# Second product of both MLPs by Strassen's scheme: seven block products for eight, z in one chunk of operands

## The chip, the cores and the metric

The kernel runs on one core of one Trainium2 chip. The metric is the device time of one execution in microseconds (us). A core has four computing engines: TensorE (PE; its weight loads are listed as PEld), VectorE (DVE), ScalarE (ACT) and GpSimd (POOL). SyncE (SP) issues most of the DMAs. Each engine executes its own instructions in the order of the program and waits on semaphores for the others. In the profile, L128 is line 128 of the kernel.

## The reference

The kernel computes a two-layer encoder trunk on x of shape (1, 512, 1024), in float32. Layer 0 has a dilated window attention as its mixer, layer 1 a short gated convolution. After each mixer stands an MLP:

```python
def mlp_sq_relu(h, w1, w2):
    return jnp.square(jax.nn.relu(h @ w1)) @ w2

for i in range(DEPTH):                      # DEPTH = 2
    y = rms_norm(h, norm1[i])
    y = mixer_a(...) if kind == 0 else mixer_b(...)
    h = h + y
    h = h + mlp_sq_relu(rms_norm(h, norm2[i]), mlp_w1[i], mlp_w2[i])
```

`w1` is 1024 x 4096 and `w2` 4096 x 1024. The change concerns the second product of the two MLPs, `z @ w2` with z = square(relu(...)).

## The kernel before

**Split operands.** A float32 factor is held as two parts of type float32r, hi (the value rounded to that type) and lo (the rest). A product is three matmuls: hi x hi, hi x lo, lo x hi, summed in PSUM. For a weight tile of 128 x 512 the pair is made on chip by `split` (lines 289 to 296): ACT casts the loaded tile `wraw` into `wh` (L292), then POOL subtracts to make `wl` (L293).

**Units and blocks.** `add_unit` (L111) describes a product of four output tiles (PSUM banks, 128 x 512) by eight k-tiles of weights (128 x 512 each). It is cut into blocks of two k-tiles. A block of a full unit is 4 tiles x 2 k-tiles x 3 = 24 matmuls; each k-tile has one load and one split. When the last matmul of a tile is issued, `done` is called, which evacuates the bank. The matmuls are those of L128.

**The order of the work.** The program is written once, by the loop at the end (lines 966 to 978). `clock` counts positions, not time: a unit of 512 columns is 8 long, a block of two k-tiles 2. Every other operation is a task at a position (`at`, and `after` for "so much after now"); tasks are issued, in order of position, between the matmuls. Within an engine that is also the order of execution. Ahead of each block the loop issues the splits of weights that lie up to six k-tiles after the block's first (`NW = 6` buffers for wh and wl) and the loads of four more (`NRAW = 4` buffers). A split therefore waits for the matmuls that last read its buffers.

```python
for i, b in enumerate(blocks):
    run_tasks(b["start"] - 0.5)
    prep_to(b["first"] + min(NW, 2 * b["n"] + i // 4))
    load_to(nprep[0] + NRAW)
    run_tasks(b["start"])
    ops = b["emit"](...)
```

**The MLP.** z has 4096 features, worked on in four chunks c of 1024. `u1(u)` is one unit of the first product: four tiles of z, 128 features x 512 tokens each. `u1_done` evacuates each: DVE multiplies relu by the norm's factor R (zr, L794), ACT squares it (zz, L795) and casts it to hi (L796), DVE subtracts for lo (L797). There are two sets of z operands, so a chunk's second product comes one chunk later than its first: u1 0 to 3, then u2 of chunk 0, u1 4 and 5, u2 of chunk 1, and so on. `u2(c, half)` is one unit of the second product, for 512 of the 1024 output features: 96 matmuls of 512 columns. `u2_done` adds its banks into the tile `acc` (L809 for the first chunk, L811 for the others). In the last chunk the sum goes to the trunk tile `hT` (L813), and `new_h` makes from it the operands and squares of the next norm (L705 to L707, L704). Before that, `acc` takes up the trunk (L850).

In layer 0 (`last` false) the weight is the stationary operand and z moves, so the output has features on the partitions. In layer 1 (`last` true) z is stationary and the weight moves, so the output has tokens on the partitions, as the result in memory wants; the trunk is transposed by 32 PE transposes (L858) and added in L860, and the output leaves by DMA from L818 and L819.

Between layers `sums` (lines 710 to 722) adds the squares over the partitions by two matmuls (L717, L718), placed 2.8 positions after the last block.

The diff touches these functions:

## Time and profile before

| | |
|---|---|
| time, median of 3 runs (lowest, highest) | 1515.11 us (1514.34, 1516.41) |
| the profiled execution, its own time | 1515.53 us |
| its span in the profile | 1513.6 us |
| busy: PE, DVE, ACT, POOL | 98%, 47%, 44%, 47% |
| second product of the MLPs, in matmuls | 2 x 768, all 128x512 |
| data read from memory | 134.89 MB |

The span is what the profile covers; the time of the profiled execution is 1.9 us more. The duration printed for a matmul overlaps its neighbours', so the time that a stream of them takes is read from the distance between starts. A line of the timeline gives the start, the duration, engine, source line, operation, output and inputs, shape and count, and in brackets how long the engine had been idle and who ended that. A line of groups gives the count, the busy time, the mean in ns of one, and the idle time before them with what ended it. A line of a stretch of time gives its length, the busy time (and count) of PE, PEld, DVE, ACT and POOL, then the granted TensorE clock, the share of the DMA engines and GB/s.

### The profile page before, as it was taken

The page shows a single profiled execution, that of the slowest core. Times are in us where ns is not written, and L with a number is a line of the kernel's source. Part 1 is how long each engine was busy: PE and PEld are TensorE (multiplying, and loading weights), DVE is VectorE, ACT ScalarE, POOL GpSimd, SP SyncE. Part 2 cuts the span into 40 slices and gives each one's busy share as a digit, 9 for nine tenths or more (in the row PEclk, how much of TensorE's full clock was granted, in tenths as well). Part 3 has the DMA queues.
Part 4 walks back from the last instruction along what each step waited for, and adds up shares of the span by engine and source line. Part 5 has one row for each costly group of instructions (what it writes and reads, how often), then busy time and mean ns, then how long its engine had stood idle before and what let it go on. Part 6 is the DMA issues. An engine that isn't in the chain of part 4 may idle for free.

```text
span 1513.6 us, 22622 instructions
## 1 busy us (share of the span) xinstructions
PE 1483.0 (98%) x7900; PEld 1293.4 (85%) x7900; DVE 706.4 (47%) x1553; ACT 664.8 (44%) x1364; POOL 716.4 (47%) x729
## 2 busy tenths in 40 slices
PE   9899999999999998999999999999999999999998
PEld 8799999999999987888888888888887888888887
DVE  4867767776767665643012223564447330122221
ACT  6456564556556564444333332433343443333320
POOL 4454444536354553554444445454454444444442
PEclk9899999999999999999999999999999999999999
DMA  6332322323132323222222232233332223222222
GB/s 151 126 112 63 102 79 86 91 75 102 53 115 60 102 84 127 103 98 96 99 97 98 91 103 96 81 90 99 98 111 84 98 92 102 97 96 94 99 90 84
DMA packets 163294, 144.77 MB, mean 96 GB/s; under 512 B 13748, under 2 KB 123116, under 8 KB 163180
## 3 DMA queue, kind: packets, MB, share of 16 engines
q1 hardware_dynamic: 162892, 143.06, 30.1%
q8 instruction: 62, 1.02, 0.3%
q14 instruction: 52, 0.43, 0.1%
q10 hardware_dynamic: 288, 0.27, 0.1%
HBM read 134.89 MB, written 8.39 MB: 95 GB/s over the span
## 4 chain that ended last, share of the span: by engine, by line
PE 77%; DVE 11%; issue 5%; POOL 3%; ACT 2%; DMA 1%; SPq 1%; POOLq 0%; ACTq 0%; DVEq 0%
PE g L128 72%; PE st L461 1%; PE o L548 1%; PE st L520 1%; PE st L391 1%; POOL wl L293 1%; DMA wraw<-in_a_wqkv 1%; DVE sm L451 1%; DVE rawA L373 1%; DVE ptl L293 1%; DVE stA L156 1%; DVE stA L155 1%; DVE sqa L704 1%; SPq L571 1%; ACT wh L292 0%
## 5 line engine op out<-in xcount | busy, mean ns | idle before, releaser
L293 POOL TENSOR_TENSOR wl<-wraw,wh 128x512 fp32r<-128x512 f32 (+1 forms) x542 | 638.2, 1198 | 712.2 <-ACT wh L292 701.2
L292 ACT CAST wh<-wraw 128x512 fp32r<-128x512 f32 (+1 forms) x542 | 300.8, 572 | 528.1 <-PE g L128 405.7
L128 PE MATMUL g<-hgBl,wh 128*128 128x512 f32 x704 | 274.8, 390 | 0.0
L128 PE MATMUL g<-hgBh,wl 128*128 128x512 f32 x704 | 274.6, 390 | 0.0
L128 PE MATMUL g<-hgBh,wh 128*128 128x512 f32 x704 | 274.6, 390 | 0.0
L128 PE MATMUL g<-wh,hgl 128*128 128x384 f32 x768 | 267.7, 349 | 0.5 <-DVE hgl L307 0.4
L128 PE MATMUL g<-wh,hgh 128*128 128x384 f32 x768 | 262.4, 342 | 1.6 <-DVE v L296 1.6
L128 PE MATMUL g<-wl,hgh 128*128 128x384 f32 x768 | 262.7, 342 | 0.0
L794 DVE SCALAR_TENSOR_TENSOR zr<-g,R 128x512 f32<-128x512 f32 x64 | 44.2, 691 | 293.4 <-PE g L128 293.3
L128 PEld LDWEIGHTS g<-hgBh,wl 128*128 128x128 f32 x704 | 132.7, 189 | 27.7
L128 PEld LDWEIGHTS g<-hgBh,wh 128*128 128x128 f32 x704 | 132.6, 188 | 27.9
L128 PEld LDWEIGHTS g<-hgBl,wh 128*128 128x128 f32 x704 | 132.7, 189 | 27.4
L128 PEld LDWEIGHTS g<-wh,hgl 128*128 128x128 f32 x768 | 145.3, 189 | 3.6 <-DVE hgl L307 1.6
L128 PEld LDWEIGHTS g<-wh,hgh 128*128 128x128 f32 x768 | 145.2, 189 | 2.7 <-DVE v L296 2.2
L128 PEld LDWEIGHTS g<-wl,hgh 128*128 128x128 f32 x768 | 144.9, 189 | 0.5
L811 DVE TENSOR_TENSOR acc<-g,acc 128x512 f32<-128x512 f32 x32 | 22.1, 692 | 138.2 <-PE g L128 138.2
L128 PE MATMUL g<-z0h,wh 128*128 128x512 f32 x192 | 74.7, 389 | 0.0
L128 PE MATMUL g<-z0l,wh 128*128 128x512 f32 x192 | 74.7, 389 | 0.0
L128 PE MATMUL g<-z0h,wl 128*128 128x512 f32 x192 | 74.7, 389 | 0.0
L470 ACT ACTIVATE sm<-sm,mxs 128x256 f32<-128x256 f32 x128 | 64.0, 501 | 15.1 <-DVE mxs L464 11.6
L292 ACT CAST pth<-st 128x512 fp32r<-128x512 f32 x64 | 37.6, 588 | 66.7 <-PE st L520 66.4
L293 DVE TENSOR_TENSOR ptl<-st,pth 128x512 fp32r<-128x512 f32 x64 | 43.5, 688 | 27.8 <-ACT pth L292 27.8
(222 smaller groups left out, 2379.0 us busy)
## 6 DMA issues: line engine op xcount, KB each, us to landing
wraw<-in_mlp_w SPq DMA_DIRECT2D x256, 256.0 KB
wraw<-in_a_wqkv SPq DMA_DIRECT2D x128, 128.0 KB
wraw<-in_a_wqkv SPq DMA_DIRECT2D x64, 192.0 KB
wraw<-in_a_wqkv SPq DMA_DIRECT2D x128, 64.0 KB
wraw<-in_b_win SPq DMA_DIRECT2D x64, 128.0 KB
v0d<-v SPq DMA_DIRECT2D x8, 512.0 KB
v<-v0d SPq DMA_DIRECT2D x64, 64.0 KB
wraw<-in_a_wo SPq DMA_DIRECT2D x16, 256.0 KB
```

The lines of the kernel that those rows point to most:

```text
L128: pe.matmul(unit["ps"][n][:, :width], a, b, start=st, stop=sp)
L155: dve.tensor_mul(t, y, y)
L156: dve.scalar_tensor_tensor(t, t, -0.5, v, op0=ALU.mult, op1=ALU.mult)
L292: act.copy(hi, src)
L293: (eng or dve).tensor_sub(lo, src, f32(hi))
L373: dve.tensor_mul(v, v, stt[:, 2, ng * r:ng * r + ng, None].to_broadcast([128, ng, 64]))
L391: pe.transpose(o, raw[r][:, w, :], ident)
L451: dve.tensor_tensor_reduce(out=sm0[:, h, b], in0=ps[h][:, 256 * b2:256 * b2 + 256], in1=msk0[:, (0, 1, 1, 2)[b]], scale=1.0, scalar=3.0e38 ...
L461: pe.matmul(pv[:, :, g], a[:, 128 * r:128 * r + 128], k[:, 256 * r:256 * r + 256], start=(q == 0), stop=(q == 2))
L470: act.activation(t[:, h, b], t[:, h, b], AF.Exp, bias=mx(m)[:, c], scale=-1.0, accum_out=mx(d)[:, c])
L794: dve.scalar_tensor_tensor(zr, ps, 0.0, state["R"], op0=ALU.max, op1=ALU.mult)
L811: dve.tensor_add(a, ps, a)
```

## The change

The second product of a chunk is a product of a 2 x 2 block matrix by another: two halves of the chunk's features (row tiles of 128 taken alternately) by two halves of the output features, and two halves of the tokens (256 each). Before, that is eight block products. The change does it by Strassen's scheme in the form with shared sums: seven block products of sums of blocks, the results added into the right output blocks.

- *Order.* A chunk is now two units of the first product and then, at once, its seven products (`add_wino`). There is one set of z operands, `zh[i]` and `zl[i]` for i = 0 to 3, each holding seven forms of 256 columns: three plain quarters and four sums. Product q uses form `OPS[q]`. Each product is two blocks, of two of the four k-tiles i, in `ORDER`: 1, 5, 1, 5, 6, 6, 2, 2, 7, 7, 3, 3, 4, 4. A block is 12 matmuls of 512 columns in layer 1 and 24 of 256 in layer 0.
- *z.* `u1_done` works on two tiles together: ACT squares into V; DVE makes four sums of 256 columns in W (`zs`, one buffer); ACT casts three quarters and then the four sums; DVE subtracts for the low part of the quarters, POOL for that of the sums.
- *Weights.* A chunk still loads 16 tiles, into twelve tiles of their own (`quad`) and four of `wraw`, and forms the sums of blocks in place by 16 DVE subtractions (`quad_make`). It splits 28 tiles, 24 with the subtraction on POOL and four on DVE.
- *Results.* Products 1, 5 and 6 are summed over the chunks in `part` and go into the trunk at the end; 2, 3, 4 and 7 are added to the trunk tile (now one tile `HT`) as they end, 7 into two blocks. `acc` is gone. Layer 1's transposes are made in its first chunk, and the trunk is kept in that form.

```diff
+    OPS = {1: 0, 6: 4, 5: 3, 2: 2, 7: 5, 3: 6, 4: 1}
+    ORDER = [(1, 0), (5, 0), (1, 1), (5, 1), (6, 0), (6, 1), (2, 0), (2, 1), (7, 0), (7, 1), (3, 0), (3, 1), (4, 0), (4, 1)]
...
+    def quad_make(q, i, raw, held):
+        a, b, c = (t[i] for t in state["quad"])
+        if q == 5:
+            dve.tensor_sub(a, b, a)
+        elif q == 6:
+            dve.tensor_sub(a, c, a)
+        elif q == 2:
+            held[i] = raw
+            return raw, (dve if i % 2 else pool)
+        elif q == 7:
+            dve.tensor_sub(b, c, b)
+            return b, pool
+        elif q == 3:
+            return c, (dve if i % 2 else pool)
+        elif q == 4:
+            d = held.pop(i)
+            dve.tensor_sub(d, d, a)
+            return d, pool
+        return a, pool
...
+    def add_wino(w, c, tok, done):
+        banks, held = {}, {}
+        for q, half in ORDER:
+            def emit(ws, q=q, half=half):
+                if half == 0:
+                    banks[q] = [ps_m(0) for _ in range(2)]
...
+                for j in range(2):
+                    ps = banks[q][j]
+                    for e, (wh, wl) in enumerate(ws):
+                        i = 2 * half + e
+                        hi, lo = state["zh"][i][:, OPS[q]], state["zl"][i][:, OPS[q]]
...
+                        if tok:
+                            ah, al = hi[:, 128 * j:128 * j + 128], lo[:, 128 * j:128 * j + 128]
+                            todo = [(ps, ah, wh), (ps, ah, wl), (ps, al, wh)]
+                        else:
+                            for n in range(2):
+                                o = ps[:, 256 * n:256 * n + 256]
+                                bh, bl = (t[:, 256 * j + 128 * n:256 * j + 128 * n + 128] for t in (wh, wl))
+                                todo += [(o, bh, hi), (o, bh, lo), (o, bl, hi)]
...
         def u1_done(u):
             def f(n, ps):
+                i = 2 * (u % 2) + n // 2
+                H, L = state["zh"][i], state["zl"][i]
                 zr = ptile(state["tp"], [128, S], F32, "zr")
                 dve.scalar_tensor_tensor(zr, ps, 0.0, state["R"], op0=ALU.max, op1=ALU.mult)
-                after(0.4, lambda: act.activation(zz, zr, AF.Square))
-                after(0.6, lambda: act.copy(hi, zz))
-                after(0.9, lambda: dve.tensor_sub(lo, zz, f32(hi)))
+                e = 2 * (n % 2)
+                if e == 0:
+                    state["zz"] = ptile(state["tp"], [128, 4, 256], F32, "zz")
+                V = state["zz"]
+                after(0.4, lambda: act.activation(V[:, e:e + 2].rearrange("p a c -> p (a c)"), zr, AF.Square))
+                if e == 0:
+                    return
+                W = ptile(state["tp"], [128, 4, 256], F32, "zs", bufs=1)
+
+                def sums_z():
+                    dve.tensor_add(W[:, 0], V[:, 0], V[:, 2])
+                    dve.tensor_sub(W[:, 1], W[:, 0], V[:, 1])
+                    dve.tensor_sub(W[:, 2], V[:, 1], V[:, 0])
+                    dve.tensor_sub(W[:, 3], V[:, 3], W[:, 1])
+                after(0.5, lambda: act.copy(H[:, 0:3], V[:, 1:4]))
+                after(0.6, sums_z)
+                after(0.75, lambda: act.copy(H[:, 3:7], W))
+                after(0.9, lambda: dve.tensor_sub(L[:, 0:3], V[:, 1:4], f32(H[:, 0:3])))
+                after(1.0, lambda: pool.tensor_sub(L[:, 3:7], W, f32(H[:, 3:7])))
             return f
...
+        def u2_done(c):
+            def f(q, j, ps):
+                part = state["part"]
+                if q in part:
+                    v = part[q][:, j]
+                    if c == 0:
+                        act.copy(v, ps)
+                    else:
+                        dve.tensor_add(v, ps, v)
+                    if c == 3 and q == 6:
+                        a1, a5 = part[1][:, j], part[5][:, j]
+                        def both():
+                            pool.tensor_add(v, v, a1)
+                            pool.tensor_add(a5, a5, v)
+                        def more():
+                            for row, col, w in ((2, 2, a5), (1, 2, a5), (2, 1, v)):
+                                o = out_block(row, col, j)
+                                dve.tensor_add(o, o, shaped(w))
+                        o = out_block(1, 1, j)
+                        dve.tensor_add(o, o, shaped(a1))
+                        after(0.1, both)
+                        after(1.0, more)
+                    return
...
-        for u in range(4):
-            u1(u)
-        u2(0, 0)
-        u2(0, 1)
...
+        for c in range(4):
             u1(2 * c)
             u1(2 * c + 1)
+            add_wino(w2[layer], c, last, u2_done(c))
```

More of the change, by code (lines that the diff above doesn't have):

```diff
@@ L136, in add_unit @@
             for kt in blk:
[L137 removed]
+                loads.append((cols, lambda kt=kt: load_raw(load, kt), lambda raw: (raw, pool)))
     ident = ptile(const, [128, 128], F32, "ident")
@@ new lines, in mlp, with turn, back @@
+        if last:
+            for f in range(2):
+                box = {}
+                def turn(r, f=f, box=box):
+                    box[r] = ps_m(0)
+                    for q in range(4):
+                        pe.transpose(box[r][:, 128 * q:128 * q + 128], state["hT"][4 * f + q][:, 128 * r:128 * r + 128], ident)
+                def back(r, f=f, box=box):
+                    dve.tensor_copy(state["hT"][4 * f + r], box[r])
+                for r in range(4):
+                    at(t0 + 9.0 + 0.5 * r + 8.0 * f, lambda r=r, turn=turn: turn(r))
+                    at(t0 + 11.0 + 0.3 * r + 8.0 * f, lambda r=r, back=back: back(r))
@@ L946, in load_to @@
             k = nload[0]
-            raws[k] = ptile(wp, [128, 512], F32, "wraw", bufs=NRAW)
-            loads[k][1](raws[k])
+            raws[k] = loads[k][1]()
             nload[0] += 1
```

131 lines of the change are left out of this document (67 added, 64 removed).

## The prediction

> **What bounds the kernel now.** I read the page's first part, then the 40 slices, the waits of TensorE and two stretches of the timeline.
>
> ```profile
> span 1513.6 us, 22622 instructions
> PE 1483.0 (98%) x7900; PEld 1293.4 (85%) x7900; DVE 706.4 (47%) x1553; ACT 664.8 (44%) x1364; POOL 716.4 (47%) x729
> PE g L717 <- ACT sgh L292: 3.3, 1, 3.3
> 672.00:715.00 43.00, 43.00 (x192) 35.59 (x191) 12.24 (x16) 18.69 (x32) 20.69 (x16) 1.00 0.29 99
> 715.00:757.00 42.00, 42.00 (x187) 34.79 (x186) 2.19 (x2) 13.92 (x24) 19.89 (x16) 1.00 0.29 100
> ```
>
> PE is the bound: 98% busy, its longest wait in the MLPs is 3.3 us before layer 1, and a stretch of first products (672 to 715) or of second products (715 to 757) has PE busy throughout at clock 1.00, POOL at half. So a matmul fewer is time saved, as long as the other engines keep PE fed. What a matmul occupies is the distance between starts, not the printed duration:
>
> ```profile
> 999.72 0.39 PE L128 MATMUL g<-hgBl,wh 128*128 128x512 f32 x1
> 1003.80 0.39 PE L128 MATMUL g<-hgBl,wh 128*128 128x512 f32 x1
> ...
> 300.94 0.34 PE L128 MATMUL g<-wl,hgh 128*128 128x384 f32 x1
> 302.32 0.34 PE L128 MATMUL g<-wh,hgh 128*128 128x384 f32 x1
> ...
> 566.31 0.30 PE L461 MATMUL st<-k1h,q1h 128*128 128x256 f32 x1
> 566.44 0.28 PE L461 MATMUL st<-k1l,q1h 128*128 128x256 f32 x1
> 566.92 0.28 PE L461 MATMUL st<-k2h,q2l 128*128 128x256 f32 x1
> ```
>
> 512 columns: 18 steps in 4.08 us, 0.2267 each. 256 columns, every one with new weights, as the change has them: 4 steps in 0.48, 0.120 each. 384 columns lie on the same line: 8 steps in 1.38, 0.1725 each.
>
> **PE's own saving.** A layer's second product is 4 chunks x 2 halves x 4 tiles x 8 k-tiles x 3 = 768 matmuls of 512: 174.1 us. In layer 0 it becomes 4 x 7 x 48 = 1344 matmuls of 256: 161.3, so 12.8 saved. In layer 1 it becomes 672 of 512: 152.3, so 21.8 saved. Together 34.6. The 256 price is bounded by 0.113 (half of 0.2267) below and by 0.13 above (the first step, 566.31 to 566.44), −9 to +13 us; I take the row, because its matmuls have the same shape. The Trainium skill (TensorE: Matmul & The Clock Gate, Back-to-back issue gap) gives N/2.4 + 2.5 ns, 109 ns for 256 columns, by which layer 0 would save 27.4. The trace disagrees: the formula gives 216 for 512, where the rows have 227.
>
> **What the other engines pay.** A chunk's weights took 16 splits (ACT cast, then POOL or DVE subtraction); now 28, with 16 DVE subtractions to form sums of blocks. A PE block has two splits and lasts 12 x 0.2267 = 2.72 us in layer 1 (24 x 0.120 = 2.88 in layer 0), half of before.
>
> ```profile
> L293 POOL TENSOR_TENSOR wl<-wraw,wh x542: 992/1288/1760, 12.6 to 1494.2; 128x512 fp32r<-128x512 f32 x96, 128x384 fp32r<-128x384 f32 x85
> 652.31 1.76 POOL L293 TENSOR_TENSOR wl<-wraw,wh 128x512 fp32r<-128x512 f32 x1
> 746.04 2.54 POOL L293 TENSOR_TENSOR wl<-wraw,wh 128x512 fp32r<-128x512 f32 x2 [2.90 <-ACT wh L292]
> L292 ACT CAST wh<-wraw 128x512 fp32r<-128x512 f32 x288 | 175.2, 621 | 400.9 <-PE g L128 360.2 <-POOL wl L293 19.8 <-DVE zr L817 7.6
> L292 ACT CAST wh<-wraw 128x384 fp32r<-128x384 f32 x254 | 125.7, 516 | 127.1 <-PE g L128 45.6 <-issue 35.6 <-DMA wraw<-in_a_wqkv 31.1
> L795 ACT ACTIVATE zz<-zr 128x512 f32<-128x512 f32 x64 | 40.5, 633 | 30.8 <-DVE zr L794 28.7
> L794 DVE SCALAR_TENSOR_TENSOR zr<-g,R 128x512 f32<-128x512 f32 x64 | 44.2, 691 | 293.4 <-PE g L128 293.3
> L902 DVE TENSOR_TENSOR z0l<-sqh,z0h 128x512 fp32r<-128x512 f32 x8 | 5.5, 693 | 5.5 <-ACT z0h L901 5.5
> L960 DVE TENSOR_TENSOR wl<-wraw,wh 128x384 fp32r<-128x384 f32 x2 | 1.1, 558 | 0.1
> L811 DVE TENSOR_TENSOR acc<-g,acc 128x512 f32<-128x512 f32 x32 | 22.1, 692 | 138.2 <-PE g L128 138.2
> 931.77 2.77 DVE L850 TENSOR_TENSOR acc<-acc,hT 128x512 f32<-128x512 f32 x2
> 418.35 3.43 DMA wraw<-in_a_wqkv
> ```
>
> Alone, a POOL subtraction takes 1.27 (2.54 for two), a DVE one 0.69. Side by side, both reading two SBUF tiles, they slow each other: POOL 1.76, DVE 1.39 (2.77 for two). DVE with a PSUM input (L811) doesn't. By the slopes between 384 and 512 columns, estimates from these rows: DVE 256 columns 0.42, 768 0.96; ACT 768 0.83, 1024 1.04; POOL 1024 2.48 (1288 plus four times 296).
>
> Loads stay 16 of 256 KB a chunk. The second block's four are held in wraw to the seventh product, so on SP's queue the next unit's loads wait for those splits; product 4's first two end 0.7 + 0.6 + 2.5 = 3.8 us after block 10 begins, a load takes up to 3.4 us more, cast and split 1.9: 9.1, and the unit begins at 10.9. So this costs nothing. The other ACT casts, DVE evacuations (16 for 8, 0.69 each in 38 us) and L850's eight adds, now gone, lie beside PE: nothing. Layer 1's transposes move a chunk earlier at the same PE cost: nothing.
>
> **The step on the path: z becomes ready too late.** Before, a chunk's z was used one pair of units later. Now the chunk's products follow its last first-product unit at once. Products 1 and 5 on k-tiles 0 and 1 (blocks 0, 1) cover it; block 2 needs the last z tile in its first form, block 3 in its sums. The queues are in order, so I walk them; T = 0 where the unit's last PSUM tile is ready, layer 1:
> - Tile 1 is ready at −2.72: zr to −2.03, square to −1.40. DVE takes tile 2's zr to −0.67, then the four sums for z tile 2 (1.70) to 1.03. ACT, in order, has the sums' cast behind them: 1.03 to 2.07. Behind it stand square 2 (2.70), block 2's two weight casts (3.94), square 3 (4.57), z tile 3's cast (5.40).
> - POOL's 1024-wide subtraction for tile 2 runs from 2.07 to 4.55, and only then come block 2's weight subtractions. The sums have one buffer, so those of tile 3 wait for it too.
> - Tile 3's sums start at 4.57 beside POOL: as many columns as two 512-wide ops, 2.8, to 7.37. Its first low part follows to 8.33. Block 2, due at 5.44, gets that at 8.33 and ends at 8.33 + 7 x 0.2267 = 9.92, where 8.16 was due.
> - The sums' cast ends at 8.41; POOL's subtraction of them takes 2.48, and 0.9 more beside DVE's two block sums, to 11.4. Block 3's two weight subtractions stand behind it: 13.15, 14.9. Block 3 needs the second for its fifth matmul and ends at 14.9 + 8 x 0.2267 = 16.7, where 10.88 was due.
> Delay: 5.8 us a chunk; in layer 0 block 3 ends at 14.9 + 16 x 0.120 = 16.8, due 11.52: 5.3. Blocks 4 and 5 then find POOL just keeping pace; blocks 6 on use one POOL split each and it gets ahead.
>
> Bounds: with no slowing at all the same walk gives sums 6.27, cast 7.31, POOL 9.79, 11.06, 12.33: delays of 3.3 and 2.7. With everything slowed, blocks 4 adds 0.8: 6.6 and 6.1. Eight chunks: 24 at least, 51 at most; I take 4 x 5.8 + 4 x 5.3 = 44, nearer the slowed end, since the same engines with the same operands are the rows above.
>
> **Smaller terms.** Last chunk of each layer: four adds on POOL at product 6's end (5.1 alone, 7 slowed) and six on DVE, beside a POOL with some 3 to 5 us of slack: 0 to 5.5, I take 2.5, so 5 for two. End of layer 0:
>
> ```profile
> 980.09 1.50 DVE L704 TENSOR_TENSOR sqa<-sqa,sqh 128x512 f32<-128x512 f32 x1
> 982.30 0.49 PE L717 MATMUL g<-sgh,ones 128*128 128x512 f32 x1
> 1508.31 0.39 PE L128 MATMUL g<-wh,z1l 128*128 128x512 f32 x1
> 1509.35 0.69 DVE L817 TENSOR_TENSOR zr<-g,acc 128x512 f32<-128x512 f32 x1 [0.66 <-DMA out<-zr]
> ```
>
> The sum of squares now ends just in time for L717 (981.6, then ACT's 0.62). Its last four tiles now come within half a block rather than over a block: about two DVE ops of 1 us later, +2 (0 to 5). At the end, 0.66 of waiting for an output buffer goes: −0.7.
>
> Sum: −34.6 + 44 + 5 + 2 − 0.7 = +16. The profiled execution took 1515.5 (span 1513.6), 0.4 above the median of the runs, 1515.1; so 1531.
>
> **The rivals.**
> *The slowing is absent: faster.* Break-even is (34.6 − 5 − 2 + 0.7) / 8 = 3.5 us of stall a chunk. Unslowed, the walk gives 3.0, and without the smaller terms the total is −34.6 + 24 − 0.7 = −11: 1504. For it: DVE and POOL overlap only in parts of the walk. Against: 1.76 and 2.77 above, and the four subtractions of tile 3 fall just on POOL's.
> *z is hidden altogether*, if the order of the queues lets tile 3 pass: −35, 1480. Against: squares and casts already stand behind weight casts today:
>
> ```profile
> 669.95 1.13 ACT L292 CAST wh<-wraw 128x512 fp32r<-128x512 f32 x2
> 670.04 0.69 DVE L794 SCALAR_TENSOR_TENSOR zr<-g,R 128x512 f32<-128x512 f32 x1
> 671.50 0.63 ACT L795 ACTIVATE zz<-zr 128x512 f32<-128x512 f32 x1
> 672.82 1.36 DVE L797 TENSOR_TENSOR z0l<-zz,z0h 128x512 fp32r<-128x512 f32 x1 [0.34 <-ACT z0h L796]
> ```
>
> The last tile's low part ends 4.1 us after its PSUM is ready, with none of the sums in it.
> *The stalls lower the clock.* Before layer 1 PE idled 3.31 us and then ran at half clock for six:
>
> ```profile
> 1160.94 0.79 PE L717 MATMUL g<-sgh,ones 128*128 128x512 f32 x1 [3.31 <-ACT sgh L292]
> 1160.00:1162.00 2.00, 1.06 (x2) 0.62 (x3) 0.93 (x2) 0.62 (x1) 0.00 (x0) 0.50 0.43 140
> 1164.00:1166.00 2.00, 2.00 (x6) 1.63 (x5) 1.90 (x4) 0.00 (x0) 0.00 (x0) 0.50 0.00 0
> 1166.00:1168.00 2.00, 2.00 (x9) 1.56 (x9) 1.90 (x4) 1.16 (x2) 0.53 (x1) 0.87 0.00 0
> ```
>
> That lost 3 us. Block 3 waits from 10.2 to 13.15, 2.9: just short. If it trips, eight times 3 more: 1555. The Trainium skill (TensorE: Matmul & The Clock Gate, Part 1) has the clock halved after an idle window of about 3.4 us; by that rule the forecast stays as it is, and the row at 3.31 agrees roughly.
>
> **How the numbers follow.** Main walk, 1520 to 1547: 0.46. Less slowing, faster, 1495 to 1511: 0.22. Hidden, 1480: 0.07. Half clock, above 1547: 0.17. Within 0.2%, about what a measurement of this kernel can tell from no change, 1512 to 1518: 0.08. So faster 0.29, same 0.08, slower 0.63. The range 1500 to 1556 leaves out the hidden case and the worst of the clock case; the main case alone is 1520 to 1547.
>
> **What would show it.** Matmuls of 256 columns start every 0.120 us. In each chunk PE waits at the third and fourth blocks, for z's low part and for wl from POOL, 5 to 6 us together, and nowhere else for long; POOL is near full from there for some 15 us with subtractions of 1.3 to 1.8. If those waits add to under 3.5 us a chunk, or 256 columns cost other than 0.12, the prediction is wrong; a clock of 0.5 after block 3 is the third rival.

## The result, and the profile after

| kernel | median of its runs (lowest, highest) | ratio to before, 95% interval |
|---|---|---|
| before | 1515.08 us (1514.34, 1516.41) | |
| changed | 1572.2 us (1569.49, 1573.13) | 1.0373 [1.0355, 1.0391] |

The change costs 57 us. The forecast had the direction (slower) and said 1531, range 1500 to 1556; the time lies 16 us above the range.

From the changed kernel's page, the span and the busy times:

```profile
span 1567.7 us, 24171 instructions
PE 1483.5 (95%) x8380; PEld 1309.3 (84%) x8380; DVE 999.9 (64%) x1885; ACT 732.3 (47%) x1456; POOL 919.3 (59%) x833
```

The four largest of its waits of TensorE (total us, times, longest):

```profile
PE g L856 <- POOL wl L299: 23.3, 26, 2.4
PE g L856 <- DVE zl L894: 14.5, 8, 2.4
PE g L724 <- ACT sgh L298: 10.4, 2, 7.1
PE g L856 <- ACT wh L298: 7.8, 3, 4.1
```

And the two stretches that were shown of before:

```profile
672.00:715.00 43.00, 39.26 (x302) 38.29 (x301) 31.94 (x32) 20.55 (x35) 36.21 (x24) 0.92 0.07 22
715.00:757.00 42.00, 42.00 (x192) 35.00 (x191) 13.75 (x19) 17.03 (x27) 26.83 (x20) 1.00 0.56 179
```

PE is still the busiest engine of the page, but it no longer works without a gap: from 672 to 715 (a chunk's products; L856) it is idle for 3.7 us and the granted clock is 0.92, while POOL, at half before, is busy for 36 of 43 us. From 715 to 757 (but for the first matmuls the units of the first product, L134) PE is busy throughout at clock 1.00, as before, and POOL and DVE have time to spare that they don't use. Among the waits of before none was in the second products; now three rows are, 45.6 us together.

The 256-column matmul in the timeline, start and printed duration:

```profile
700.02 0.28 PE L856 MATMUL g<-zh,wh 128*128 128x256 f32 x1
...
702.90 0.28 PE L856 MATMUL g<-zh,wh 128*128 128x256 f32 x1
```

24 steps in 2.88 us: 0.120 each, as forecast. Call the usual distance between starts the pitch (0.2267 us for 512 columns, 0.120 for 256). Over the whole of the MLPs and the conv, every microsecond beyond it can be put down as a stall or, where a distance is about twice the pitch, as half clock:

| us beyond the pitch | before | changed | forecast for the difference |
|---|---|---|---|
| ends of units, 8 chunks: stalls | 0 | 45 | 44 |
| ends of units: half clock | 0 | 14 | 0 (a rival: 24) |
| rest of the two last chunks | 0 | 22 | 5 |
| after layer 0 (L717, now L724) | 0.7 | 9.5 | 2 |
| elsewhere | 7.7 | 7.6 | |
| sum | 8.4 | 98.1 | |

The difference, 89.7, less the 34.6 that the pitches save PE, is 55.1; the spans differ by 54.1, of which the tail behind the last matmul takes −0.6 (5.29 us before, 4.69 now).

One unit's end in layer 1, the second chunk, in the timeline: the waits of PE, then DVE, then POOL.

```profile
1331.39 0.50 PE L856 MATMUL g<-wl,zh 128*128 128x512 f32 x1 [0.44 <-POOL wl L299]
1333.21 0.50 PE L856 MATMUL g<-wh,zl 128*128 128x512 f32 x1 [1.32 <-DVE zl L894]
1337.72 0.50 PE L856 MATMUL g<-wl,zh 128*128 128x512 f32 x1 [2.40 <-POOL wl L299]
1339.40 0.79 PE L856 MATMUL g<-wl,zh 128*128 128x512 f32 x1 [0.72 <-POOL wl L299]
...
1328.69 1.50 DVE L887 TENSOR_TENSOR zs<-zz 128x256 f32<-128x256 f32 x1 [2.14 <-POOL zl L895]
1333.08 3.47 DVE L813 TENSOR_TENSOR wa<-wb,wa 128x512 f32<-128x512 f32 x2
...
1326.25 2.41 POOL L895 TENSOR_TENSOR zl<-zs,zh 128x1024 fp32r<-128x1024 f32 x1 [3.28 <-PE g L856]
1333.44 2.55 POOL L895 TENSOR_TENSOR zl<-zs,zh 128x1024 fp32r<-128x1024 f32 x1 [2.11 <-ACT zh L893]
1335.95 6.33 POOL L299 TENSOR_TENSOR wl<-wa,wh 128x512 fp32r<-128x512 f32 x4
```

A stretch of 2 us behind it (the granted clock, 0.50, is the figure after POOL's busy time):

```profile
1340.00:1342.00 2.00, 2.00 (x6) 1.61 (x5) 2.00 (x3) 0.62 (x1) 2.00 (x2) 0.50 0.00 0
```

This is the forecast's walk: DVE's sums of z (L887) wait for POOL's wide subtraction (L895), POOL stands idle 2.11 us for ACT's cast of the sums, and the weight subtractions (L299) come behind the second L895; PE waits at the third block for z's low part and at the fourth for wl. New is the end: after idles of 1.32, 2.40 and 0.72 the clock is 0.50.

A last chunk (layer 0), PE, DVE and POOL, and the sum of squares after it:

```profile
980.60 0.58 PE L856 MATMUL g<-zh,wh 128*128 128x256 f32 x1 [4.13 <-ACT wh L298]
...
970.75 4.04 DVE L930 TENSOR_TENSOR hT<-hT,part 128x512 f32<-128x512 f32 x3
977.32 1.90 DVE L930 TENSOR_TENSOR hT<-hT,part 128x512 f32<-128x512 f32 x3 [2.53 <-POOL part L925]
979.13 1.29 DVE L820 TENSOR_TENSOR wb<-wc,wb 128x512 f32<-128x512 f32 x2
...
974.20 1.73 POOL L924 TENSOR_TENSOR part<-part,part 128x512 f32<-128x512 f32 x1
976.01 1.27 POOL L925 TENSOR_TENSOR part<-part,part 128x512 f32<-128x512 f32 x1
...
1013.36 0.79 PE L724 MATMUL g<-sgh,ones 128*128 128x512 f32 x1 [7.06 <-ACT sgh L298]
```

The trunk's adds of the part sums (L930) take 4.04 us for three, then wait 2.53 for POOL, and product 7's weight sums (L820) stand behind them: their cast comes so late that PE idles 4.13.

Two of DVE's sums of z, of which L889 has no POOL work beside it, and POOL's subtractions (count, busy us, mean ns):

```profile
L887 DVE TENSOR_TENSOR zs<-zz 128x256 f32<-128x256 f32 x32 | 30.9, 964 | 34.2 <-POOL zl L895 34.2
L889 DVE TENSOR_TENSOR zs<-zz 128x256 f32<-128x256 f32 x32 | 13.3, 416 | 0.0
L299 POOL TENSOR_TENSOR wl<-wa,wh 128x512 fp32r<-128x512 f32 x96 | 137.2, 1454 | 16.1 <-ACT wh L298 14.7
```

### The profile page after: what moved, and what is told of

It reads as the page before. It is cut to its first block, busy times and chain, and to the rows that moved or that the text cites. A ratio compares the mean times of both kernels' runs of the same rounds, so it can differ in the third digit from the quotient of the medians.

```text
span 1567.7 us, 24171 instructions
## 1 busy us (share of the span) xinstructions
PE 1483.5 (95%) x8380; PEld 1309.3 (84%) x8380; DVE 999.9 (64%) x1885; ACT 732.3 (47%) x1456; POOL 919.3 (59%) x833
## 4 chain that ended last, share of the span: by engine, by line
PE 67%; DVE 16%; POOL 7%; issue 5%; ACT 3%; DMA 1%; SPq 1%; ACTq 0%; POOLq 0%; DVEq 0%
PE g L134 48%; PE g L856 13%; POOL wl L299 4%; POOL zl L895 2%; PE o L554 2%; PE st L467 1%; PE st L397 1%; PE st L526 1%; DVE sm L457 1%; ACT wh L298 1%; DVE sqa L711 1%; DVE ptl L299 1%; DVE rawA L379 1%; DVE rawB L379 1%; DMA wraw<-in_a_wqkv 1%
## 5 line engine op out<-in xcount | busy, mean ns | idle before, releaser
L299 POOL TENSOR_TENSOR wl<-wraw,wh 128x384 fp32r<-128x384 f32 (+1 forms) x462 | 542.8, 1197 | 436.2 <-ACT wh L298 427.1
L298 ACT CAST wh<-wraw 128x384 fp32r<-128x384 f32 (+1 forms) x478 | 258.5, 563 | 299.6 <-PE g L134 114.0
L134 PE MATMUL g<-hgBl,wh 128*128 128x512 f32 x704 | 275.6, 392 | 0.0
L134 PE MATMUL g<-hgBh,wh 128*128 128x512 f32 x704 | 275.3, 391 | 0.0
L134 PE MATMUL g<-hgBh,wl 128*128 128x512 f32 x704 | 275.0, 391 | 0.0
L134 PE MATMUL g<-wh,hgl 128*128 128x384 f32 x768 | 267.6, 348 | 0.4 <-DVE hgl L313 0.2
L134 PE MATMUL g<-wh,hgh 128*128 128x384 f32 x768 | 262.5, 342 | 2.5 <-DVE v L302 2.5
L134 PE MATMUL g<-wl,hgh 128*128 128x384 f32 x768 | 262.6, 342 | 0.0
L134 PEld LDWEIGHTS g<-hgBh,wl 128*128 128x128 f32 x704 | 133.0, 189 | 27.8
L134 PEld LDWEIGHTS g<-hgBh,wh 128*128 128x128 f32 x704 | 132.8, 189 | 27.7
L134 PEld LDWEIGHTS g<-hgBl,wh 128*128 128x128 f32 x704 | 133.0, 189 | 27.3
L134 PEld LDWEIGHTS g<-wh,hgh 128*128 128x128 f32 x768 | 145.2, 189 | 3.5 <-DVE v L302 3.1
L134 PEld LDWEIGHTS g<-wh,hgl 128*128 128x128 f32 x768 | 145.2, 189 | 3.3 <-DVE hgl L313 1.4
L299 POOL TENSOR_TENSOR wl<-wa,wh 128x512 fp32r<-128x512 f32 x96 | 137.2, 1454 | 16.1 <-ACT wh L298 14.7
L134 PEld LDWEIGHTS g<-wl,hgh 128*128 128x128 f32 x768 | 144.8, 189 | 0.5
L856 PE MATMUL g<-zh,wl 128*128 128x256 f32 x448 | 133.2, 297 | 9.0 <-POOL wl L299 8.9
L856 PE MATMUL g<-zl,wh 128*128 128x256 f32 x448 | 131.5, 293 | 9.5 <-DVE zl L894 9.5
L895 POOL TENSOR_TENSOR zl<-zs,zh 128x1024 fp32r<-128x1024 f32 x32 | 78.2, 2444 | 102.1 <-ACT zh L893 77.4
L856 PE MATMUL g<-zh,wh 128*128 128x256 f32 x448 | 131.1, 293 | 4.1 <-ACT wh L298 4.1
L856 PE MATMUL g<-wl,zh 128*128 128x512 f32 x224 | 95.2, 425 | 14.8 <-POOL wl L299 14.3
L298 ACT CAST wh<-wa 128x512 fp32r<-128x512 f32 x96 | 58.1, 618 | 101.9 <-DVE wa L813 63.0
```

The lines of the kernel that those rows point to most:

```text
L134: pe.matmul(unit["ps"][n][:, :width], a, b, start=st, stop=sp)
L298: act.copy(hi, src)
L299: (eng or dve).tensor_sub(lo, src, f32(hi))
L856: pe.matmul(o, st, mv, start=s0, stop=s1)
L895: after(1.0, lambda: pool.tensor_sub(L[:, 3:7], W, f32(H[:, 3:7])))
```

## The experiments

All times, each with its ratio to runs of before on the same chip:

| run | us | ratio [95%] |
|---|---|---|
| e1_cover4 | 1581.67 | 1.0445 [1.043, 1.0461] |
| e2_no_sums | 1515.44 | one run |
| e3_filler | 1569.38 | 1.0355 [1.0338, 1.0373] |
| e4_ends | 1570.18 | 1.0366 [1.035, 1.0381] |
| e5_low_on_dve | 1555.39 | 1.0271 [1.0257, 1.0285] |
| e6_cover4_low_on_dve | 1563.23 | 1.0316 [1.0302, 1.033] |
| e7_combined | 1547.34 | 1.0216 [1.0202, 1.023] |
| e8_no_parts | 1590.31 | 1.0507 [1.0491, 1.0522] |
| e9_no_parts_lead9 | 1559.49 | 1.0302 [1.0287, 1.0318] |
| e10_combined_lead9 | 1565.27 | 1.0341 [1.0324, 1.0358] |
| e11_deferred_adds | 1525.77 | 1.0074 [1.0057, 1.0091] |
| e12_z_later | 1533.65 | 1.0124 [1.0106, 1.0142] |
| e13_best_order | 1519.92 | 1.0038 [1.0023, 1.0053] |
| e14_best_no_wsums | 1481.98 | 0.9788 [0.9773, 0.9803] |
| e15_change_no_wsums | 1544.31 | 1.0199 [1.0182, 1.0216] |
| e16_free_chain | 1515.77 | 1.0011 [1.0002, 1.002] |
| e17_bank_earlier | 1523.39 | 1.006 [1.0047, 1.0072] |

### Four first tries: z, the clock, the ends (e1 to e4)

**e1**: more cover for z. The first halves of four products (they need only z tiles 0 and 1) stand ahead of all second halves.

```diff
-    ORDER = [(1, 0), (5, 0), (1, 1), (5, 1), (6, 0), (6, 1), (2, 0), (2, 1), ...
+    ORDER = [(1, 0), (5, 0), (6, 0), (2, 0), (1, 1), (5, 1), (6, 1), (2, 1), ...
```

> All the work is done; only the order changes: the first halves of products 1, 5, 6 and 2 run before any second half, so that four blocks (10.9 to 11.5 us) and not two stand between the last z tile and its first reader. Layer 1's transposes move some positions earlier so that PSUM banks suffice. Theory A (z's last tile comes late through the queues in order, and PE waits for it): the changed kernel's waits of 45 us at the eight unit ends and the 14 us of half clock behind them go, save about 1 us a chunk for block 2's weights, which still stand behind z's 1024-wide subtraction on GpSimd: about 1572 - 59 + 8 = 1521 us. Theory B (preparing 28 weight tiles for 36 to 40 us of matmuls is too slow whatever z does): the waits move to later blocks of the same stretch and most of the 59 us stay: 1550 us or more.

It was slower, 1581.67. The timeline of POOL at a unit's end, with PE's longest wait there:

```profile
1335.09 2.40 POOL L895 TENSOR_TENSOR zl<-zs,zh 128x1024 fp32r<-128x1024 f32 x1 [3.28 <-PE g L856]
1343.66 2.36 POOL L895 TENSOR_TENSOR zl<-zs,zh 128x1024 fp32r<-128x1024 f32 x1 [2.12 <-ACT zh L893]
1347.74 0.79 PE L856 MATMUL g<-wl,zh 128*128 128x512 f32 x1 [3.09 <-POOL wl L299]
```

Theory A's 1521 is refuted. Nobody waits for z now, but POOL's queue is the same: L895 stands in it, idle 3.28 and 2.12 us, ahead of weights that PE needs. The waits for wl rose from 23.3 to 45.7 us. So a later reader of z is not enough; the weights stand behind z's tasks. The order has a price of its own, too (e6).

**e2** leaves out z's sums, their cast and the wide subtraction, and the products read the plain quarters instead, so the output is not the MLP's; weights, splits and the number of matmuls stay.

> Leaves out the four sums of z: no sums on VectorE, no 1024-wide cast, no 1024-wide subtraction on GpSimd; the products use the three plain quarters instead, with the same matmuls and all 28 weight preparations. Theory A: z tile 3 is squared and split without waiting, block 2 and block 3 find it and their weights in time; waits and half clock at the unit ends fall from 59 us to under 12: about 1525 us. Theory B: weights are prepared as before and the waits for wl stay: 1555 us or more.

1515.44 in its one run: 57 us less than the changed kernel, and theory B, which put e1 right, is refuted. Its waits:

```profile
PE g L724 <- ACT sgh L298: 10.7, 2, 7.4
PE g L856 <- POOL wl L299: 6.3, 10, 1.1
PE g L856 <- ACT wh L298: 5.8, 3, 2.8
```

The chunks 0 to 2 of layer 0 have no stall left, with all 28 splits and 16 weight sums in place. So at the unit ends the weights alone keep pace; what is left is mostly in the last chunks (21 us) and at L724, some 35 us beyond before's by the distances, which PE's 34.6 just pay.

**e3**: useless matmuls fill PE's idle time before blocks 2 and 3, so that the clock stays up.

```diff
+                    ops[at_op:at_op] = [lambda: pe.matmul(banks[0], g[:, 0:128], g, start=True, stop=True)] * k
```

> Adds matmuls of no use into a spare PSUM bank just ahead of the matmuls that wait in blocks 2 and 3 (10 and 5 of 512 columns in layer 0, 6 and 10 in layer 1, not in layer 1's first chunk), 15 or 16 a chunk, 3.4 to 3.6 us of PE time, as long as the waits there. If half of the cost behind the waits is the clock (14 us at the unit ends by the matmuls' distances), keeping PE busy saves most of it: about 1572 - 10 = 1562 us and a granted clock of 1.00 after block 3. If the clock fell for another reason, or its loss is hidden behind the weights, the time stays at 1572 or rises by up to 10.

Half clock at the unit ends went from 14 to 4.5 us, the time by 2.8, with intervals that overlap. The half clock falls where PE would wait for weights anyway: taken away, it comes back as a wait (for wl still 21.7 us, beside some 24 us of useless matmuls where PE had waited). By itself it is worth at most some 3 us of the 57.

**e4**: the trunk's adds of the parts 0.6 block later, the conv's sum of squares two blocks later.

```diff
-                        after(1.0, more)
+                        after(1.6, more)
-    add_sums(clock[0] + 2.0)
+    add_sums(clock[0] + 4.0)
```

> All the work is done; two places change. In the last chunk the three trunk additions of products 1, 5 and 6 come 0.6 positions later, behind the next weight sums on VectorE, and the sums for the norm after layer 0 come two positions later. If the last chunk's waits (16 us with the clock) come from weight sums that stand behind these additions, and those at the end of layer 0 (9.5 us) from squares that come too late, about 6 and 7 us go: 1559 us. If they come from GpSimd's part additions and from VectorE's load alone, under 4 us go in all: 1568 or more.

2 us less, with intervals that overlap: the side of POOL's adds and DVE's load. L724's waits fell from 10.4 to 4.5 us (3.3 of them at layer 1's start, as before), but the rest came back as waits of the conv's first blocks, and the last chunks got no better: POOL was busy from 966 to 987 but for one wait of 1.36 us.

### Head-of-line blocking on POOL (e5 to e7)

The theory now: POOL's queue is in order, and L895 waits in it for ACT's cast, ahead of weights that are ready. **e5** moves only that instruction.

```diff
-                after(1.0, lambda: pool.tensor_sub(L[:, 3:7], W, f32(H[:, 3:7])))
+                after(1.0, lambda: dve.tensor_sub(L[:, 3:7], W, f32(H[:, 3:7])))
```

> The changed kernel with one edit: the 1024-wide subtraction for the low part of z's sums is on VectorE (1.22 us by the slope) and not on GpSimd (2.4 us). Theory C, formed from the two runs before: what keeps PE waiting is that this subtraction stands in GpSimd's order ahead of the weights, waits there for ScalarE's cast and then takes 2.4 us, so that weights come late wherever z is read. Then blocks 2 and 3 get their weights sooner, 2 to 3 us a chunk: 1572 - 20 = 1552 us. Theory A (z's chain through ScalarE and VectorE alone, with GpSimd's queue without part in it): VectorE gets longer by 2.4 us a chunk, 1572 to 1585.

1555.39, 17 us less, where theory C had 20. The longest wait for wl fell from 2.4 to 1.1:

```profile
PE g L856 <- POOL wl L299: 20.6, 26, 1.1
PE g L856 <- ACT wh L298: 12.9, 11, 4.2
PE g L856 <- DVE zl L894: 9.5, 7, 1.4
```

The waits together are hardly shorter, since more of them are now for ACT's wh. By the distances the products lose 67 us where they lost 82: 9.5 of the gain is half clock that no longer comes after the shorter idles, 5.6 is stalls.

**e6** is e1 and e5 together.

> The four-block cover (first halves of products 1, 5, 6 and 2 before any second half) together with the 1024-wide subtraction on VectorE. Theory C: with GpSimd's queue free of z and z read late, the waits at the unit ends mostly go, but for products 5 and 6 whose weight sums hang on the product just before them: about 10 to 15 us left of the 60: 1530 us. Theory B (weights too slow in any order): 1555 or more.

A miss, in the rival's range: 1563.23. Waits for wl were 33.7 us, 52 of them, longest 2.2. By the timeline products 5 and 6 come so close here that the in-place weight sum of one waits for the split of the other, and DVE's z tasks stand ahead of the sums. It is 8 us over e5, as e1 is 9.5 over the changed kernel: e1's order costs that, wherever L895 stands, and L895's move is worth 17 to 18 us in either order.

**e7** puts together: the order 1, 2, 5, 3 by first halves, then second halves, then 6, 7, 4 (plain weights first); L895 on DVE; the parts of the first three chunks folded into the trunk after the third, so that the last chunk has no fold.

> All the work is done. The order in a chunk is first halves of 1, 2, 5, 3, then their second halves, then 6, 7, 4, so that no weight sum hangs on the product just before it and z's sums are read first in the seventh block; the 1024-wide subtraction is on VectorE; the sums of products 1, 5 and 6 over chunks 0 to 2 go into the trunk during the units after, and in the last chunk every product is added from PSUM into its blocks; the sums after layer 0 come one position later. Theory C: waits at the unit ends under 1.5 us a chunk (12), at the last chunk's end 3 us a layer (6), after layer 0 about 6: 1514 - 34.6 + 24 = 1504 us, faster than both kernels. If the 28 splits and 16 weight sums are too much for VectorE and GpSimd side by side in 36 us, waits of 3 us and more a chunk remain, late in each chunk, and it is at or above 1515.

1547.34, not 1504. DVE, ACT and POOL at a unit's end:

```profile
761.95 1.22 DVE L895 TENSOR_TENSOR zl<-zs,zh 128x1024 fp32r<-128x1024 f32 x1
763.08 1.29 DVE L813 TENSOR_TENSOR wa<-wb,wa 128x512 f32<-128x512 f32 x2
...
763.86 1.23 ACT L298 CAST wh<-wa 128x512 fp32r<-128x512 f32 x2 [1.68 <-DVE wa L813]
...
764.55 2.71 POOL L299 TENSOR_TENSOR wl<-wa,wh 128x512 fp32r<-128x512 f32 x2 [9.17 <-ACT wh L298]
```

POOL is idle 9.17 us, at the end because the weights' next step (L813) stands behind z's tasks on DVE, the last of them L895. The blocking has moved from POOL to DVE; how much of the 9.17 the short lead takes is not told apart here.

### Lead (e8 to e10)

Weights are prepared three blocks ahead (six pairs `wh`, `wl`). Three more pairs take 12 KB of a partition, as much as `part`, which is given up for them: every product is added from PSUM into all the blocks that it feeds. **e8** does that alone, **e9** adds the pairs, **e10** both to e7. In e8 and e9 product 1 of layer 1's first chunk is added to trunk tiles that are turned only afterwards; the instructions are the same in number and kind.

```diff
-    state["part"] = ...
+        FEEDS = {1: ((1, 1), (1, 2), (2, 1), (2, 2)), 2: ((1, 1),), 5: ((1, 2), (2, 2)), 6: ((1, 2), (2, 1), (2, 2)), ...
+                for row, col in FEEDS[q]:
+                    dve.tensor_add(o, shaped(ps), o)
...
-    NW = 6
+    NW, NX = 6, 3      # e9, e10: three more pairs in the MLPs
```

> The three part sums are gone: products 1, 5 and 6 are added from the accumulators straight into the trunk blocks that they feed, 28 accumulator adds a chunk on DVE for 16, and no part adds behind the last product 6 on GpSimd and DVE. It is the control for the next two. Theory D (the extra 22 us in the two last chunks come from the part adds: two a half on GpSimd, among the weight subtractions, and three a half on DVE, which wait for them): the last chunks lose some 14 us less, 1572 - 14 = about 1558. Rival R (it is the rate of weight work there, whoever does the adds, and in the other six chunks 12 more accumulator adds of 0.68 us, 8.2 us a chunk, stand ahead of the weight sums in DVE's order): the gain in the last chunks is given back, 1568 or more.

> As the run without part sums, and the 12 KB of a partition that these leave hold three more pairs of split weights: within the MLPs nine pairs for six, so that weights are worked four and a half blocks ahead for three. Theory E (the weight waits at a unit's end are a want of lead: GpSimd and DVE are half idle in the units before and may not work ahead): the waits of the second product for GpSimd's low weights and ACT's high weights (31 us together) fall below 10 us, those for z's low parts (14.5 us) stay; about 25 us less than the run without part sums. Rival B (rate: 28 splits and 16 sums a chunk at contended prices do not fit beside the blocks of 2.7 to 2.9 us): the wait only moves some blocks later, less than 8 us gained on the run without part sums.

> The combined version (order 1, 2, 5, 3 by first halves, then second halves, then 6, 7, 4; the wide subtraction of z on DVE), with no part sums and nine pairs of split weights. The combined version took 1547 with waits of 33 us for GpSimd's low weights left. Theory E: these fall below 12 us and the kernel takes 1510 to 1522, about the kernel before or a little under it by the remainder. Rival B: the waits stay above 25 us, 1538 or more.

e8, 1590.31: the rival's time, 18 us more than the changed kernel. Of these 7.8 are one wait of layer 1's transposes for product 1's adds; the other chunks before the last lose up to 5 us more each by the distances, with twelve more adds on DVE ahead of weight sums. But theory D's part holds as well: the two last chunks lose 24.6 us where they lost 36.6, and no more than their neighbours (layer 0: 11.6 beside 11.3 to 11.5). So the extra loss of the last chunk comes from the fold of the part sums. e9 took 30.8 off e8 (25 expected), and its waits for POOL's low weights are 1.7 us in all: lead it is, for the weights; what is left at the unit ends are z's waits, 16.7 us for ACT's cast and 16.0 for DVE's low part. e10, 1565.27, is in the rival's range and no gain on e7, though the waits for low weights fell from 33.1 to 24.4 us. DVE and ACT:

```profile
786.85 4.86 DVE L928 TENSOR_TENSOR hT<-g,hT 128x512 f32<-128x512 f32 x8
...
792.42 1.20 ACT L298 CAST wh<-wa 128x512 fp32r<-128x512 f32 x2 [4.78 <-DVE wa L815]
```

Product 1's eight adds stand between two weight sums of product 6 (L815), and ACT's cast waits 4.78 for the second.

### Order on DVE, and the two halves of the cost (e11 to e15)

**e11** spreads the adds over the blocks that follow, lets the three further pairs come into use one by one, and issues the conv's sum of squares 1.5 blocks later, which is too late: the conv's first outputs take a stale scale. **e12** sets that right, makes z tiles 2 and 3 later, uses the further pairs only near the second products, and spreads more of the last chunk's adds; **e13** is e12 with z at its earlier time.

```diff
+                        after((0.53 if j == 0 else 1.6 if q == 1 and c < 3 else 0.2) + 0.4 * n, lambda rc=rc: feed(*rc))
```

> As the combined version with nine pairs and no part sums, with three changes of order only: a product's accumulator adds are spread over the next one to three blocks, each behind the weight sums of the block after (in the run before, eight of them, 4.86 us, stood in DVE's order ahead of product 6's weight sums, ACT's casts waited 3.32 and 4.78 us for those, and the blocks of product 6 lost some 6 us a chunk and 1.5 to 2 at half clock); the three further pairs come into use one after the other from the third unit on (in the run before, ACT stood 5.1 us ahead of the squares' cast for weights whose transfers had not landed); the conv's sum of squares is issued 1.5 blocks later. Theory F (what is left of the change's loss is order within DVE's and ACT's queues): 1565 - 8 x 6 to 7.5 - 6 - 4 = 1497 to 1510, under the kernel before. Rival B (the rate of DVE and GpSimd on weights, whose instructions take 1.3 to 2.2 times as long side by side, cannot follow blocks of 2.7 to 2.9 us): the waits move to the blocks of products 6, 7 and 4 and 1540 or more is left.

> The version of the run before with four more moves: the operands of z's third and fourth part (needed four blocks after a unit's end in this order) are made 0.9 and 1.8 blocks later, so that the weight sums of products 5 and 6 come ahead of them in DVE's order; the three further pairs are used only within three blocks of the second product, so that the sums' cast does not stand behind weights that still travel; the conv's sum of squares goes back to 0.8 blocks after its earlier place (in the run before, at 2.5, it came too late for the conv's first outputs, which took a stale scale: that run's output differed, its order of work did not); and in the last chunk only products 7 and 4 are added at once. Theory F (order within DVE's and ACT's queues): the run before took 1525.8 with some 2.5 to 4 us lost a chunk, 6 at each last chunk and 7.5 after layer 0; half to three quarters of that goes, 1498 to 1512, no slower than the kernel before (1514). Rival B (the rate of weight work): the late operands of z push the weights of products 7 and 4 back, 1522 or more.

> The run before (order by first halves, no part sums, nine pairs near the second product, adds spread) with z's operands made at their earlier time again. Delaying them cost 8 waits of up to 1.2 us for z's wide low part and won nothing: so 1534 - 8 x 1.2 = about 1524 under the theory that order decides; 1532 or more if the weight work's rate takes back whatever is given to it.

e11 took 40 us off e10: 1525.77, still above the 1510 expected. e12, 1533.65, came out in the rival's range: z later only made z late (eight waits for its wide low part, up to 1.2 us). e13 is 1519.92, the side of order, a little under the 1524 expected. So lead, order and L895's place together take back all but 0.4% over before, of 3.7%; no run tells their shares apart with 16 adds a chunk.

**e14** leaves the weight sums out of e13, **e15** out of the changed kernel.

```diff
         if q == 5:
-            dve.tensor_sub(a, b, a)
...
         elif q == 7:
-            dve.tensor_sub(b, c, b)
```

> The same with the 16 in-place weight sums a chunk left out (every product takes the plain quarters as they were loaded, so the output is not the reference's; products, splits, z's operands and adds are all there). Theory G (the rest of the loss is the weight sums, their 1.3 to 1.8 us beside GpSimd and the chain through them): 1485 to 1500, what 34.6 us off the kernel before with some 10 us of other loss gives. Rival H (the rest is z's operands and the spread adds): 1512 or more.

> The changed kernel as it stands with the 16 in-place weight sums a chunk left out (every product takes a plain quarter, so the output is not the reference's). Its partner is the run without z's sums, which took 1515. Theory C and G together (at a unit's end z's tasks and the weights share the queues, and either one alone fits): the waits for GpSimd's low weights at the unit ends go, those for z's low parts (14.5 us) stay, and the last chunks lose less: 1520 to 1535. Rival H (z's tasks alone make the loss, the weight sums only stand beside it): 1555 or more.

e14: 1481.98, theory G's side, just under its range. With no weight sums the kernel is 31.4 us faster than before. By the distances its second products have no stall at all, and its stalls and half clock elsewhere are within 2 us of before's: the saving of PE, forecast as 34.6, is there. e15 fell between the two expectations, 1544.31: the weight sums are 28 us of the changed kernel, z's sums (e2) 57. With the weight sums alone (e2) the unit ends have no stall; with z's sums alone (e15) z's own waits stay, 14.5 us, and those for wl fall from 23.3 to 16.1. So at the unit ends z's sums make most of the loss and the weight sums lengthen it. No run of the changed kernel leaves out both, so the two savings may not be added.

### Chain or rate (e16, e17)

In e13 one stall a chunk was left, ahead of product 6. It was taken for a wait for product 6's fourth weight, whose in-place sum overwrites a tile that product 5 had split. **e16** forms the same sums another way, so that none overwrites a tile that was split just before; it also spreads product 1's adds a little further and takes the conv's first weights in another order.

```diff
-    ORDER = [(1, 0), (2, 0), (5, 0), (3, 0), (1, 1), (2, 1), (5, 1), (3, 1), (6, 0), (6, 1), (7, 0), (7, 1), (4, 0), (4, 1)]
+    ORDER = [(2, 0), (3, 0), (7, 0), (1, 0), (1, 1), (2, 1), (3, 1), (7, 1), (6, 0), (6, 1), (4, 0), (4, 1), (5, 0), (5, 1)]
...
         if q == 5:
-            dve.tensor_sub(a, b, a)
+            dve.tensor_sub(a, c, a)
         elif q == 6:
-            dve.tensor_sub(a, c, a)
+            dve.tensor_add(a, a, b)
```

> The best order so far with another way to the same seven products: order 2, 3, 7, 1 by first halves, 1, 2, 3, 7 by second halves, then 6, 4, 5; the weight sums are b = c - b for product 7, a = a + b for 6, d = d - a for 4, a = c - a for 5. They are as many as before, 16 a chunk on DVE, but none overwrites a quarter that a product of the block just before has yet to split: product 7's wait for nothing but transfers, 6's, 4's and 5's each come four blocks or more behind the split that they overwrite. Splits, adds, z's operands and transfers are as before. Theory K (the chain: one stall a chunk at product 6's fourth weight, 1.6 us with its like in layer 0 and 2.8 to 3.0 with half clock behind it in layer 1, 25 us in all): 1492 to 1502, under the kernel before. Rival B (rate): the stall moves to products 4 and 5, 1515 or more.

1515.77, ratio 1.0011: even with before, but not the 1492 to 1502 of the chain theory. PE's waits in layers 0 and 1:

```profile
864.77 0.36 PE L858 MATMUL g<-zh,wh 128*128 128x256 f32 x1 [0.95 <-DVE hT L930]
1229.73 0.47 PE L858 MATMUL g<-xwh,zh 128*128 128x512 f32 x1 [2.17 <-DVE hT L930]
```

They are waits for a bank (an accumulator in PSUM), free only after product 2's add. So was e13's stall, though its row names ACT:

```profile
1233.50 0.47 PE L856 MATMUL g<-xwh,zh 128*128 128x512 f32 x1 [2.83 <-ACT wh L298]
1233.47 0.19 PEld L856 LDWEIGHTS g<-xwh,zh 128*128 128x128 f32 x1 [3.23 <-issue]
1227.70 2.83 POOL L299 TENSOR_TENSOR xwl<-wa,xwh 128x512 fp32r<-128x512 f32 x2 [1.34 <-ACT xwh L298]
1232.86 0.62 ACT L298 CAST wh<-wb 128x512 fp32r<-128x512 f32 x1 [1.08 <-DVE wb L820]
1229.83 1.25 DVE L815 TENSOR_TENSOR wa<-wc,wa 128x512 f32<-128x512 f32 x1
1231.00 1.75 DVE L820 TENSOR_TENSOR wb<-wc,wb 128x512 f32<-128x512 f32 x1
1232.67 3.07 DVE L928 TENSOR_TENSOR hT<-g,hT 128x512 f32<-128x512 f32 x5
```

But PE's weight load begins at 1233.47, before that cast ends, and the cast is of product 7's first weight. Product 6's first two weights (xwh, xwl) were ready at 1230.53. What ends just before the load is the first of DVE's five adds, at 1233.35, product 2's, and it stood behind two weight sums. All eight stalls of e13 at this place have an add of DVE ending some 0.1 us before the load. So the chain that e16 took apart was not the cause: the fourth weight's sum (L815) waits for nothing there, DVE simply comes to it late. e16 shortened the same bank wait (layer 0: 1.8 to 1.1 us, layer 1: 3.0 to 2.3). **e17** frees it a block earlier by swapping two second halves.

```diff
-    ... (1, 0), (1, 1), (2, 1), (3, 1), ...
+    ... (1, 0), (2, 1), (1, 1), (3, 1), ...
```

> As the run before, with the second half of product 2 ahead of product 1's, so that product 2's adds are issued a block earlier and product 6, which takes its bank, does not wait for them; and product 1's adds are spread in the last chunk as in the others. Theory L (the bank is what the waits name: 3 x 0.94 in layer 0, 3 x 2.17 with some half clock in layer 1, and some 3 us in the last chunks): 1500 to 1508, faster than the kernel before. Rival B in its last form (DVE's rate: 38 us of work without a gap in the 38 to 41 us of a chunk's products): the waits pass to the next thing that DVE makes, a weight sum or another bank, 1512 or more.

1523.39: the bank's waits are gone and those for weights are back (for wl 8.9 us, in e16 3.7). The reason stands in 40 us of the third chunk of layer 0, counted from each kernel's own start of the products; DVE's busy time is the third after the length (37.52). e13, with the weight sums:

```profile
843.00:883.00 40.00, 38.03 (x311) 37.38 (x310) 37.52 (x49) 16.59 (x28) 25.67 (x17) 1.00 0.03 11
```

e14, without them:

```profile
836.00:876.00 40.00, 40.00 (x335) 39.96 (x334) 28.35 (x43) 20.48 (x33) 32.73 (x25) 1.00 0.18 58
```

e16:

```profile
841.00:881.00 40.00, 38.29 (x318) 37.91 (x317) 38.70 (x51) 18.28 (x30) 28.65 (x20) 1.00 0.08 27
```

e17:

```profile
842.00:882.00 40.00, 38.54 (x310) 38.04 (x309) 39.08 (x48) 17.70 (x29) 28.71 (x19) 0.97 0.08 27
```

DVE is busy for 37.5 to 39.1 of 40 us with the weight sums and 28.4 without. Over the whole products of a chunk it is busy in e16 for 39.4 to 40.7 us, where the matmuls by their pitch take 40.3 in layer 0 and 38.1 in layer 1. So in these versions DVE's rate bounds a chunk's products, and whatever is put first, something else that DVE makes is late. That holds for them, with 28 adds a chunk. The changed kernel has 16, and over a chunk's products its DVE and POOL are busy for 35 to 38 of 46 to 47 us (the last chunks apart); there the runs point to order and lead. No run has 16 adds and nine pairs, so whether that would pass before stays open.

## Why the prediction was right or wrong

The direction and the largest term were right. What failed are three smaller steps of the sum: the last chunks, put at 5 us, cost 22; the end of layer 0, put at 2, cost 8.8; half clock, put at nothing, cost 14.

- **What bounds the kernel, and PE's saving: right.** The pitch of 256 columns is 0.120. e14 shows the saving in the time: 31.4 us, with 2 us more of stalls than before.
- **z late at the unit ends, 44: right in place and size.** 45 us of stalls, at the third block for z's low part and the fourth for wl, in the order of the walk. In the chunk shown, counted from the start of its products (1324.02), z's low part is there at 9.2 and the fourth block's second wl at 15.4, where the walk has 8.33 and 14.9. The price that the term rests on, engines side by side at 1.39 (DVE) and 1.76 (POOL), was low for DVE: 1.73 for 512 columns (two of L813 in 3.47), 1.50 for 256 (L887), where 0.42 is the price alone.
- **Half clock, 0: a step that failed.** The forecast kept it as a rival (1555), since the idle before block 3 was put just short of the one row that it had (3.31 us). It trips after 2.4 us, and at 1.3 and 2.4 together. In the distances it is 14 us; e3 shows that by itself it is worth at most some 3.
- **The last chunks, 5: the step that failed by most, 22.** The forecast priced the adds as work beside a POOL with slack, and counted six on DVE where a layer has eight (L930 and L932). In the trace DVE's adds wait for POOL (2.53 us) with product 7's weight sums behind them. It has nothing to do with z, since without z's sums (e2) these chunks still lose 21 us; it is the fold of the part sums, since without it (e8) they lose no more than their neighbours. e4 shows that moving the adds alone doesn't help: POOL and DVE have hardly any slack there.
- **After layer 0, 2: mis-sized, 8.8.** Two DVE ops late was the estimate; L724 waited 7.06. The trunk adds, the four last tiles and the conv's weights are in one pair of queues; that these together make the wait is argued, not shown: e4 moved the sums back and part of the loss came up in the conv's first blocks.
- **The tail, −0.7: right**, −0.6.
- **The rivals.** "The slowing is absent" is refuted by the groups above, "z is hidden" by the waits for zl, 14.5 us; and e1 shows that even with z covered the weights behind it are late. Main case and clock case came together, and the range had them only one at a time. The chance for slower, 0.63, was on the right side; the upper end missed the two terms at the ends of the layers, 24 us.

So the miss of 41 is 14 for half clock, 17 for the last chunks, 7 after layer 0 and 1 at the unit ends; the other 2 are there because the profiled execution (1569.49) was the fastest, 2.7 below the median. These are places, not causes that add up: e3 shows that half clock and late weights cover each other.

## What to carry to other kernels

A saving on the bounding engine is worth what the helpers can still feed in the shorter block: count, for the stretch after each hand-over and not for the span, what each in-order queue must do there and how many blocks ahead it may work; here PE's blocks were halved, the lead stayed at three blocks, and POOL, half idle over the span before, was busy for 36 of 43 us. An instruction that waits for another engine, put into a queue ahead of work that is ready, holds that work up for its wait and its own time: one such subtraction moved to the producer's side gave 17 us, 2.1 a chunk. Look, where a wait is named, at whether the named instruction ended before the waiting one began: e13's label named a bystander, and e16 took apart a chain that nobody waited for. And price a helper's instruction by a row that shows it beside its neighbour, at every place where they meet, the rare ones (last chunk, end of layer) too.

## What the hardware showed

- DVE and POOL, each with two operands in SBUF, slow each other more than the trace of before showed: DVE's 512 columns take 0.69 alone and 1.73 beside POOL (L813, two in 3.47); 256 columns 0.42 (L889) and 1.50 (L887); POOL's 512 columns 1.27 and 1.73 (L925, L924). DVE with a PSUM operand stays at 0.68 (the adds of e13, mean 675 ns). The Trainium skill (SBUF — State Buffer, SBUF: two separate sides) has the two arbitrate for one pair of ports that the loser must wait for during the whole instruction; 0.69 + 1.27 = 1.96 would then be a pair, as an estimate, and where both work without a gap each takes some 1.73, so the rows agree roughly.
- The clock fell after shorter idles than the one row of before, 3.31. Layer 0's first chunk, the wait and a stretch behind it:

```profile
678.26 0.39 PE L856 MATMUL g<-zl,wh 128*128 128x256 f32 x1 [2.38 <-DVE zl L894]
```

```profile
680.00:682.00 2.00, 1.47 (x7) 1.17 (x6) 2.00 (x2) 0.31 (x1) 2.00 (x2) 0.50 0.00 0
```

Some 2 us after an idle of 2.38 it is 0.50. The Trainium skill (TensorE: Matmul & The Clock Gate, Part 1) puts an idle window at about 3.4 us; here shorter idles, one or several close together, were enough.
